# w_up's product by Strassen's seven block products, and w_down as a stage of its own

## Chip and metric

One core of a Trainium2 chip runs one inference step of a decoder layer. The metric is the time of an execution on the device in microseconds. A profile was taken of one further execution; its span, from the first to the last recorded instruction, is what the trace's times count in.

## The reference

Two groups of tokens share the weights: 1024 prompt tokens and 8 x 4 sample tokens, 1056 in all, with 1024 features. Everything is float32. The change concerns the feed-forward part, with d_ff = 2816:

```python
x = x + (g_a * y_a + g_b * y_b + g_m * y_m) @ w_o
h = _rmsnorm(x, norm_ffn_g) @ w_up                        # 1024 -> 2 * 2816
hc, conv_f_state = _causal_dwconv3(h, conv_f_prev, conv_f_w)
hc = hc + conv_f_b
a, gt = jnp.split(hc, 2, axis=-1)
x = x + (jax.nn.silu(gt) * a) @ w_down                    # 2816 -> 1024
```

The convolution runs over three tokens; each sample sequence has two cached rows in front of its four tokens. The final norm follows. Outputs are the normed x and several states, among them the last two rows of h.

## The kernel before

Features lie on the 128 partitions and tokens on the columns. 1056 token columns are cut into three chunks of 352. A float32 operand is kept as two parts of a rounded type (fp32r): hi, which ScalarE casts (L199), and lo, the remainder, which VectorE subtracts (L201). A product is three matmuls for each 128 contracted features (`three`, L221): hi by hi, hi by lo, lo by hi, summed in PSUM.

Weights come in units of 512 KB (8 contracted tiles x 128 columns, or 4 x 256): SP loads one into `ws` (three buffers, L177), it is split into `wh` and `wl`, and `next_unit` and `ahead` (L205, L215) keep up to two split and four loaded ahead. `main` (L239) takes one unit and runs `chunk` (L226) for the three chunks: 24 matmuls of 352 columns into a PSUM tile `mm` (three buffers), then an evacuation by a function that the caller gives. Other work (norms, gates, transposes) is queued in `aux` and woven in between the chunks, by `pace` and `weave` (L99 to L112). Each engine executes its instructions in the order in which the program records them; no scheduler moves them.

The stages around the change are these:

- w_o: 8 units; the first four by `main`, the last four (kept in `kept`) chunk by chunk (L1225 to L1233). `wo_evac` (L1211) adds x, and sums the squares into `acc`. After each chunk its norm (`norm2`, L1196, with `column_norm`, L256) is woven into the next one: a sum over features by PE, a scaling of 8 blocks on VectorE, hi on ScalarE, lo on VectorE and GpSimd in turn.
- w_up: for each of 22 feature tiles j the tile of a and that of the gate, 44 units in all (L1311). `up_evac` (L1243) copies the chunk out of PSUM to `hb`, computes the convolution's centre tap on ScalarE (L1272) and the two others on VectorE (L318), applies the sigmoid (L1280), and the products and the split into hi and lo follow on VectorE and ScalarE (`gate`, L1253).
- w_down: as soon as four tiles j are gated (after j = 4, 8, 12, 16; two after 18), `down_group` (L1296) multiplies them by their rows of w_down and adds the result to S on VectorE (L1294). The last four run at the end in column pieces of 384, 416 and 256, each followed by its final norm and its stores (`finish`, L1345), so that only the last piece's norm is left after the last matmul.

In the w_up part GpSimd sets two zero columns, copies cached columns, and copies the last rows of h (L323, L324, L330, L331). `S` holds x, transposed; `zhi` and `zlo` the parts of the normed x; `fs` and `rs` are pools of 9 and 8 slots of 1088 columns.

Of the kernel before, what the change touches and what calls it, by code (L numbers as in the profile page):

```python
# [31 lines left out]
class Slots:  # L32


    def __init__(self, pool, n, dtype, name):
        self.free = deque(
            pool.tile([P, SLOT], dtype, name=f"{name}{i}", tag=f"{name}{i}") for i in range(n)
        )

    def get(self):  # L40
        return self.free.popleft()

    def put(self, *tiles):
        self.free.extend(tiles)
# [11 lines left out]
def layer_step(ctx: ExitStack, tc: tile.TileContext, I, O):  # L56
# [73 lines left out]
    DOWN = {4: (0, 4), 8: (4, 4), 12: (8, 4), 16: (12, 4), 18: (16, 2)}  # L130
# [24 lines left out]

    def down_units(j0, nk):
        w = 1024 // nk
        for q in range(D // w):
            unit_cols(w_down, q * w, k0=j0, nk=nk, cols=w)

    for j in range(NJ):
        unit_cols(w_up, j * P)
        if j in DOWN:
            down_units(*DOWN[j])
        unit_cols(w_up, FF + j * P)
    for c in range(3):
        down_units(18, 4)
# [199 lines left out]
    with tc.manual_schedule():  # L367
        slots = ctx.enter_context(tc.tile_pool(name="slots", bufs=1))
        fs = Slots(slots, 9, F32, "fs")
        rs = Slots(slots, 8, F32R, "rs")  # L370
# [823 lines left out]
        acc, sqs = fs.get(), fs.get()  # L1194

        def norm2(c):  # L1196
            def sums(ms):
                b = bank()
                for i in range(3):
                    t0, n = PIECES[3 * c + i]  # L1200
                    mmul(b[:n, i : i + 1], lhsT=acc[:, t0 : t0 + n], rhs=ones[:, 0:1], start=True, stop=True)
                for i, n in ((slice(0, 2), P), (slice(2, 3), CH - 256)):
                    nc.vector.tensor_copy(out=ms[:n, i], in_=b[:n, i])
                if c == 2:
                    fs.put(acc)

            total, spread, scales = column_norm(c, G_FFN, sums)
            no = lambda: None
            return [no] * 3 + [total] + [no] * 4 + [spread] + scales

        def wo_evac(f):  # L1211
            def go(c, r, ps):
                until(lambda: c in back)
                nc.vector.tensor_tensor(out=S[:, f, r], in0=ps, in1=S[:, f, r], op=ALU.add)
                if f == 0:
                    nc.scalar.activation(out=acc[:, r], in_=S[:, f, r], func=AF.Square)
                else:
                    i = (f + c) % 3
# [6 lines left out]
        for f in range(4):  # L1225
            main(wo_evac(f))
# [10 lines left out]
        for i in list(kept):  # L1237
            rs.put(*kept.pop(i))
# [222 lines left out]
```

## Time and profile before

| what | value |
|---|---|
| median of 3 runs | 1913.81 us (1911.98 to 1915.22) |
| the profiled execution | 1912.15 us, span 1910.1 us |
| granted TensorE clock | 0.996 of full |
| w_o's matmuls | from about 1034 us |
| w_up and w_down, mixed | about 1129 to 1899 us |
| DMA | 160 MB, mean 84 GB/s |

A row of a group reads: line, engine, operation, result <- operands, shape, count, then busy time and mean length of one in ns, then the idle time of its engine just before and what ended it. A row of the timeline has the start and the length in us first. Lengths of matmuls overlap, as they are pipelined; the distance between two starts is what one costs in a stream. Lengths of VectorE, ScalarE and GpSimd include some start and end that can overlap with the neighbours'. The windows view has the stretch, its length, then busy time of PE, PEld (weight loads), DVE (VectorE), ACT (ScalarE) and POOL (GpSimd), each with a count, the granted clock, the busy share of the DMA engines and GB/s.

### The profile page before, as it was taken

To read this page: it belongs to the slowest core of one execution; us is meant where nothing else is said; L and a number is where in the kernel's file an instruction comes from. 1 tells how busy PE (TensorE), PEld (TensorE's weight loads), DVE (VectorE), ACT (ScalarE), POOL (GpSimd) and SP (SyncE) were. 2 spreads that over 40 slices of the span, in tenths; PEclk is the share of its full clock that TensorE was granted. 3 is DMA by queue.
4 is the path that set the end of the run, shared out by engine and by line. 5 is a ranking of instruction groups with operands and counts; after the bars stand their busy time and mean duration, and the time that the engine had idled before them with its cause. 6 is when DMAs were issued, how large, how long until landed. Compare 5 with 4: busy or idle time off the path is not lost.

```text
span 1910.1 us, 29127 instructions
## 1 busy us (share of the span) xinstructions
PE 1878.9 (98%) x11844; PEld 1856.4 (97%) x11844; DVE 1040.7 (54%) x2274; ACT 631.7 (33%) x1231; POOL 123.8 (6%) x322
## 2 busy tenths in 40 slices
PE   8999999999999999999999999999999999999998
PEld 8988999999999999999999999999999999999997
DVE  5576775336633483329435267546546546556666
ACT  6654313211231123221324144414324324222444
POOL 2231100000000000000000131000000000000000
PEclk9999999999999999999999999999999999999999
DMA  8736152125211432133215001111111111111123
GB/s 263 208 102 219 57 191 67 56 67 167 67 58 45 135 99 70 45 114 119 78 47 181 23 12 56 46 45 45 49 42 45 58 43 46 46 45 48 44 78 135
DMA packets 204851, 160.45 MB, mean 84 GB/s; under 512 B 5477, under 2 KB 191405, under 8 KB 204717
## 3 DMA queue, kind: packets, MB, share of 16 engines
q1 hardware_dynamic: 194660, 144.76, 24.8%
q10 hardware_dynamic: 10057, 13.84, 2.1%
q8 instruction: 93, 1.52, 0.3%
q14 instruction: 41, 0.34, 0.1%
HBM read 144.98 MB, written 13.59 MB: 83 GB/s over the span
## 4 chain that ended last, share of the span: by engine, by line
PE 86%; DVE 7%; issue 3%; ACT 2%; DMA 0%; POOL 0%; DVEq 0%; ACTq 0%; POOLq 0%
PE mm L224 26%; PE mm L222 26%; PE mm L223 26%; DVE qr L855 2%; DVE wl L201 1%; DVE fs L318 1%; PE acc L913 1%; ACT wh L199 1%; PE aux L985 0%; PE aux L986 0%; PE mm L803 0%; PE aux L223 0%; PE aux L984 0%; PE aux L222 0%; PE aux L224 0%
## 5 line engine op out<-in xcount | busy, mean ns | idle before, releaser
L222 PE MATMUL mm<-zhi,wh 128*128 128x352 f32 x2880 | 933.4, 324 | 0.3 <-ACT zhi L284 0.3
L223 PE MATMUL mm<-zlo,wh 128*128 128x352 f32 x2880 | 930.9, 323 | 1.0 <-POOL zlo L295 1.0
L224 PE MATMUL mm<-zhi,wl 128*128 128x352 f32 x2880 | 930.5, 323 | 0.2 <-DVE wl L201 0.2
L222 PEld LDWEIGHTS mm<-zhi,wh 128*128 128x128 f32 x2880 | 542.8, 188 | 1.2 <-ACT zhi L284 0.6
L223 PEld LDWEIGHTS mm<-zlo,wh 128*128 128x128 f32 x2880 | 541.9, 188 | 1.9 <-POOL zlo L295 1.6
L224 PEld LDWEIGHTS mm<-zhi,wl 128*128 128x128 f32 x2880 | 542.0, 188 | 0.5 <-DVE wl L201 0.5
L201 DVE TENSOR_TENSOR wl<-ws,wh 128x1024 fp32r<-128x1024 f32 x181 | 226.6, 1253 | 146.7 <-ACT wh L199 146.5
L199 ACT CAST wh<-ws 128x1024 fp32r<-128x1024 f32 x182 | 190.5, 1049 | 337.8 <-PE mm L223 315.9
L318 DVE SCALAR_TENSOR_TENSOR fs<-fs,vec,fs 128x352 f32<-128x352 f32 (+2 forms) x416 | 199.4, 492 | 98.6 <-ACT fs L1272 88.8
L222 PE MATMUL mm<-rs,wh 128*128 128x352 f32 (+3 forms) x528 | 172.1, 326 | 2.1 <-DVE S L1294 2.1
L223 PE MATMUL mm<-rs,wh 128*128 128x352 f32 (+3 forms) x528 | 171.1, 324 | 0.0
L224 PE MATMUL mm<-rs,wl 128*128 128x352 f32 (+3 forms) x528 | 170.9, 324 | 0.0
L1294 DVE TENSOR_TENSOR S<-mm,S 128x352 f32<-128x352 f32 (+3 forms) x144 | 75.1, 523 | 124.2 <-PE mm L224 124.0
L855 DVE CUSTOM_DVE_ANT_0 qr<-fs,fs 128x256 f32<-128x256 f32 x256 | 108.5, 424 | 7.3
L222 PEld LDWEIGHTS mm<-rs,wh 128*128 128x128 f32 x528 | 99.1, 188 | 3.2 <-ACT fs L360 1.7
L223 PEld LDWEIGHTS mm<-rs,wh 128*128 128x128 f32 x528 | 99.3, 188 | 0.5 <-DVE rs L1261 0.3
L224 PEld LDWEIGHTS mm<-rs,wl 128*128 128x128 f32 x528 | 99.0, 188 | 0.2
L1139 ACT ACTIVATE sig<-mm 128x352 f32<-128x352 f32 x72 | 33.5, 465 | 187.7 <-PE mm L224 187.3
L1271 ACT COPY fs<-mm 128x352 f32<-128x352 f32 (+2 forms) x176 | 62.2, 380 | 91.7 <-PE mm L224 85.1
L1272 ACT ACTIVATE fs<-mm,vec 128x352 f32<-128x352 f32 x132 | 86.7, 656 | 0.0
L1152 DVE TENSOR_TENSOR sig<-sig,fs 128x352 f32<-128x352 f32 x48 | 25.2, 525 | 108.0 <-ACT sig L1139 108.0
L1280 ACT ACTIVATE fs<-fs 128x352 f32<-128x352 f32 x66 | 32.9, 498 | 98.2 <-DVE fs L318 98.1
(235 smaller groups left out, 1561.0 us busy)
## 6 DMA issues: line engine op xcount, KB each, us to landing
ws<-in_w_in SPq DMA_DIRECT2D x88, 512.0 KB
ws<-in_w_up SPq DMA_DIRECT2D x44, 512.0 KB
fs<-q_d SPq DMA_DIRECT2D x32, 512.0 KB
ws<-in_w_down SPq DMA_DIRECT2D x30, 512.0 KB
fs<-in_cache_mem_k SPq DMA_DIRECT2D x16, 512.0 KB
fs<-in_cache_mem_v SPq DMA_DIRECT2D x16, 512.0 KB
xT_d<-S ACTq DMA_DIRECT2D x3, 1408.0 KB
S<-xT_d ACTq DMA_DIRECT2D x6, 704.0 KB
```

Source lines behind the costliest of these rows:

```text
L199: nc.scalar.copy(out=hi, in_=t)
L201: lows.append(lambda: eng.tensor_tensor(out=lo, in0=t, in1=f32(hi), op=ALU.subtract))
L222: mmul(ps, lhsT=wh, rhs=xh, start=first, stop=False)
L223: mmul(ps, lhsT=wh, rhs=xl, start=False, stop=False)
L224: mmul(ps, lhsT=wl, rhs=xh, start=False, stop=last)
L318: nc.vector.scalar_tensor_tensor(out=dst, in0=src(k), scalar=col(w0 + k * step), in1=dst, op0=ALU.mult, op1=ALU.add)
L855: nc.vector.tensor_tensor_reduce(out=att["qr"], in0=q[:, i, :], in1=t[:, 2 * (bb % 2) + mt, :], scale=1.0, scalar=0.0, op0=ALU.mult, op1=A ...
L1139: nc.scalar.activation(out=t, in_=ps, func=AF.Sigmoid)
L1271: nc.scalar.copy(out=dst, in_=src)
L1272: nc.scalar.activation(out=o[:, r], in_=ps, func=AF.Identity, scale=col(CFW + 88 + i), bias=col(CFB + i))
L1280: nc.scalar.activation(out=hold["s"][:, r], in_=o[:, r], func=AF.Sigmoid)
L1294: nc.vector.tensor_tensor(out=S[:, f, r], in0=ps, in1=S[:, f, r], op=ALU.add)
```

## The change

**w_up.** The tokens are cut into four quarters of 264 columns. The weights of an entry are a 2 x 2 block matrix: rows are the tile of a and the tile of the gate of the same j, columns are the two halves of the contracted features (four tiles each). The input is one too: its rows are the two halves of the features, its columns the quarters s and s + 2, with s = 0 or 1. Strassen's scheme, in its form with 15 sums, gives the four output blocks with seven products, numbered 1 to 7 and run in the order 1, 6, 2, 5, 7, 3, 4. One product is 12 matmuls of 264 columns (4 tiles x 3). There are 24 entries: j = 0 and 1 are run for s = 0 alone, then both for s = 1 (entries 0 to 3); from j = 2 on an entry runs both.

- Input sums: `norm2(s)` scales the four blocks, forms four differences of 4 x 264 columns on GpSimd and splits seven operands of that size: hi on ScalarE, lo for six on VectorE and for product 4's on GpSimd. `norm2(0)` is woven into the second half of w_o, `norm2(1)` into entries 0 and 1.
- Weight sums: `w_sum` makes four sums of 512 columns on GpSimd for each entry, three before product 6 and one before product 3; `prepare` casts on ScalarE and takes the lo part on VectorE, or for products 2 and 4 on GpSimd. It runs three products ahead.
- Outputs: `evacuate` adds a product's PSUM tile to a running sum in `S`; seven kinds of additions of 264 columns, 14 on VectorE for a full entry, two copies on ScalarE. `S` is free for this since x goes to DRAM (`x_d`).
- Convolution and gate are done over all 1056 columns at once, as eight `late` items that run during the next entry: for each half centre (ScalarE, with four small GpSimd copies) and two taps (VectorE), then sigmoid (ScalarE, with the product of gate and a on GpSimd) and the gate's last product (VectorE), which is stored to DRAM (`act_d`).

**w_down** begins when w_up is done. For each quarter the gated features are read back from DRAM and split, and for each of four column groups of w_down all 22 tiles are summed in PSUM: w_down is read four times. `finish` takes a quarter in three pieces of 88 tokens.

```diff
+        ORDER = (1, 6, 2, 5, 7, 3, 4)
+        entries = [(0, (0,)), (1, (0,)), (0, (1,)), (1, (1,))] + [(j, (0, 1)) for j in range(2, NJ)]
...
+        def w_sum(e, n):
...
+            if n == 6:
+                tt(out=s1, in0=a21, in1=a22, op=ALU.add)
+                tt(out=s2, in0=s1, in1=a11, op=ALU.subtract)
+                tt(out=a21, in0=a11, in1=a21, op=ALU.subtract)
+                return s2
+            if n == 3:
+                tt(out=a11, in0=a12, in1=s2, op=ALU.subtract)
+                return a11
+            return {2: a12, 5: s1, 7: a21, 4: a22}[n]
...
+        def prepare(upto):
+            while prepared[0] < min(upto, len(steps)):
...
+                a = w_sum(e, n)
+                t = ring.tile([P, KT, P], F32R, name="wh", tag=("wh", "wl")[prepared[0] % 2], bufs=3)
+                hi, lo = t[:, 0:4, :], t[:, 4:8, :]
+                nc.scalar.copy(out=hi, in_=a)
+                eng = nc.gpsimd if n in (2, 4) else nc.vector
+                eng.tensor_tensor(out=lo, in0=a, in1=f32(hi), op=ALU.subtract)
+                wform[e, n] = hi, lo
+                if n == 3 and e + 1 < len(entries):
+                    raw_load(e + 1)
...
+            def sigmoid():
+                s = block(S, j % 2, 1)
+                g = outs[j, 1]
+                nc.scalar.activation(out=s, in_=as4(g), func=AF.Sigmoid)
+                nc.gpsimd.tensor_tensor(out=g[:, :T], in0=g[:, :T], in1=outs[j, 0][:, :T], op=ALU.mult)
+
+            def gate():
+                g, s = outs.pop((j, 1)), block(S, j % 2, 1)
+                nc.vector.tensor_tensor(out=as4(g), in0=as4(g), in1=s, op=ALU.mult)
+                nc.sync.dma_start(out=act_d[j], in_=g[:, :T])
...
+        def product(e, n, s):
+            wh, wl = wform[e, n]
+            ps = banks[s] = bank("mm" if s else "aux")[:, :QC]
+            xh, xl = forms[n, s]
+            for k in range(4):
+                three(ps, wh[:, k, :], wl[:, k, :], xh[:, k, :], xl[:, k, :], k == 0, k == 3)
...
-        for j in range(NJ):
...
+        for at, (e, n) in enumerate(steps):
...
+            prepare(at + 4)
...
+            for _ in range(2 if n == 1 else 1):
+                if late:
+                    late.popleft()()
+            for _ in range(2 if e < 2 else 1):
+                if aux:
+                    aux.popleft()()
+            for s in ss:
+                product(e, n, s)
+            for s in ss:
+                evacuate(e, n, s)
...
+            if 1 in ss:
+                if n == 3:
+                    late.extend(conv_items(j, 0))
+                if n == 4:
+                    late.extend(conv_items(j, 1) + gate_items(j))
...
+        for c in range(4):
...
             for q in range(4):
-                w = next_unit()
+                ps = [bank("mm")[:, :QC] for _ in range(2)]
+                for g in range(6):
+                    wh, wl = next_unit()
+                    ahead()
+                    until(lambda: (c, g) in homes)
```

The next rows are the order of VectorE's queue before, for the second unit of a pair in w_up: L318 are taps, L1256 and L1257 the gate's products, L1261 the low part of the gated features, L201 that of a weight unit.

```order
L318 SCALAR_TENSOR_TENSOR fs_98<-fs_97,vec,fs_98 128x352 x2
L1256 TENSOR_TENSOR fs_98<-fs_98,fs_96 128x352
L1257 TENSOR_TENSOR fs_98<-fs_98,fs_99 128x352
L1261 TENSOR_TENSOR rs_108<-fs_98,rs_110 128x352
L318 SCALAR_TENSOR_TENSOR fs_98<-fs_97,vec,fs_98 128x352 x2
```

And this is VectorE's queue now, in an entry of the later part, from the last tap of the entry before (L1389, L1393) on: L1426 evacuates products 5, then 7, then 3; L1341 are the low parts of the next entry's product 1 (from `ws`) and 6 (from the sum in `S`); L1411 is the gate.

```order
L1389 SCALAR_TENSOR_TENSOR rs_13045<-rs_12912,vec,rs_13045 128x1024
L1393 SCALAR_TENSOR_TENSOR rs_13045<-ext,vec,rs_13045 128x32
L1426 TENSOR_TENSOR S<-aux,S 128x264
L1426 TENSOR_TENSOR S<-mm,S 128x264
L1341 TENSOR_TENSOR wh<-ws,wh 128x512
L1426 TENSOR_TENSOR rs_13181<-aux,S 128x264
L1426 TENSOR_TENSOR S<-aux,S 128x264
L1426 TENSOR_TENSOR rs_13181<-mm,S 128x264
L1426 TENSOR_TENSOR S<-mm,S 128x264
L1341 TENSOR_TENSOR wh<-S,wh 128x512
L1411 TENSOR_TENSOR rs_13045<-rs_13045,S 128x1056
L1426 TENSOR_TENSOR rs_13113<-aux,S 128x264
```

The low part of product 6 stands ahead of the gate and of the evacuations of product 3, and it takes its operand from GpSimd's sum. GpSimd's queue in the same part of w_up was this, for one unit and the beginning of the next:

```order
L323 MEMSET fs_97 128x2
L324 COPY fs_97<-hal_f 128x8x2
L330 COPY tail_f_115<-fs_97 128x2
L331 COPY tail_f_115<-fs_97 128x16
L323 MEMSET fs_103 128x2
```

Now it holds, for an entry, the sum for product 3 (L1325), the low part of 4 (L1341), the product of gate and a (L1407), the three sums for product 6 (L1320 to L1322), the low part of 2 (L1341), and the small copies:

```order
L1325 TENSOR_TENSOR ws<-ws,S 128x512
L1357 MEMSET rs_13113 128x2
L1341 TENSOR_TENSOR wh<-ws,wh 128x512
L1407 TENSOR_TENSOR rs_13045<-rs_13045,fs_12966 128x1056
L1357 MEMSET rs_13181 128x2
L1320 TENSOR_TENSOR S<-ws 128x4x128
L1321 TENSOR_TENSOR S<-S,ws 128x4x128
L1322 TENSOR_TENSOR ws<-ws 128x512
L1341 TENSOR_TENSOR wh<-ws,wh 128x512
L1371 COPY ext<-hal_f 128x8x2
```

What moved: GpSimd's four small operations of a unit became seven operations over 512 or 1056 columns with the small ones beside them, and the sums for product 6 stand behind the product of the entry before, which waits for the sigmoid and so for VectorE's last tap.

More of the change, by code (lines that the diff above doesn't have):

```diff
@@ L1194, in layer_step @@
         acc, sqs = fs.get(), fs.get()
-        def norm2(c):
-            def sums(ms):
-                b = bank()
[L1199 to L1204, printed above, removed]
-                    fs.put(acc)
-            total, spread, scales = column_norm(c, G_FFN, sums)
-            no = lambda: None
-            return [no] * 3 + [total] + [no] * 4 + [spread] + scales
+        QC = 264
@@ new lines, in gate_items @@
+        def gate_items(j):
+            def sigmoid():
[7 more added lines that the diff above has]
+                nc.sync.dma_start(out=act_d[j], in_=g[:, :T])
+                fs.put(g, outs.pop((j, 0)))
+                if j % 4 == 3:
+                    for half in range(2):
+                        aux.append(lambda i=j - 3 + half * NJ, x=2 * half + j // 4 % 2: tail_rows(tail_f[x], i, 4, pf, sf))
+            return [sigmoid, gate]
@@ new lines, in layer_step @@
+        for i, c in enumerate((0, 2, 1, 3)):
+            r = quarter(c)
+            for half in range(2):
+                for f in range(4, 8):
+                    if half == 0:
+                        if f == 4:
+                            nc.sync.dma_start(out=x_d[c, :, 0:4, :], in_=S[:, 0:4, r])
+                        wh, wl = wo[f]
+                        ps = bank("mm")[:, :QC]
+                        for k in range(KT):
+                            three(ps, wh[:, k, :], wl[:, k, :], zhi[:, k, r], zlo[:, k, r], k == 0, k == KT - 1)
+                            if k == 3:
+                                weave()
+                        wo_evac(f)(r, ps)
+                        weave()
+                        nc.sync.dma_start(out=x_d[c, :, f, :], in_=S[:, f, r])
+            if i == 1:
+                prepare(1)
+                aux.extend(norm2(0) + [lambda: prepare(3)])
+                pace(15)
@@ L1337, in layer_step @@
-        for half in range(2):
-            aux.append(lambda i=20 + half * NJ, s=4 + half: tail_rows(tail_f[s], i, 2, pf, sf))
-        gfin = fs.get()
-        nc.sync.dma_start(out=gfin[:, :D], in_=I["norm_final_g"].partition_broadcast(P))
-        nc.scalar.activation(out=one, in_=one, func=AF.Sqrt)
-        def finish(a0, a1, end):
-            rows = [(t, min(P, NP - t)) if t < NP else (t, T - NP) for t in range(a0, a1, P)]
-            banks, ys, sums = {}, {}, {}
+        fs.free.extend(rs.free)
@@ L1349, in finish @@
+        def finish(c, end):
+            rows = [(c * QC + i * 88, 88) for i in range(3)]
+            y = [block(S, h, c) for h in range(2)]
+            banks, yo, sums = {}, {}, {}
             ms, r, tmp = (small.tile([P, 4], F32, name=n, tag=n, bufs=2) for n in ("ms4", "tmp4", "y4"))
@@ L1380, in out @@
                 fr = slice(half * 512, (half + 1) * 512)
[L1381 removed]
+                y, b, ri = yo[i][:n, fr], banks.pop((i, half))[:n, :], r[:n, i : i + 1]
                 if dve:
@@ L1417, in layer_step @@
         drain()
-        for i in range(2):
+        for i in range(3):
             turn(i, 1)()
-        scales(0, 2)
-        for i in range(2):
+        scales(0, 3)
+        for i in range(3):
             out(i, 0, True)
-            out(i, 1, i == 1)
+            out(i, 1, i == 2)
 _INS = [
```

453 lines of the change are left out of this document (311 added, 142 removed).

## The prediction

> **What bounds the kernel now.** I read the page's shares first, then its chain of waits, then the stretch of the FFN in the windows view.
>
> ```profile
> PE 1878.9 (98%) x11844; PEld 1856.4 (97%) x11844; DVE 1040.7 (54%) x2274; ACT 631.7 (33%) x1231; POOL 123.8 (6%) x322
> PE 86%; DVE 7%; issue 3%; ACT 2%; DMA 0%; POOL 0%; DVEq 0%; ACTq 0%; POOLq 0%
> ```
> ```profile
> 1129.00:1892.00 763.00, 760.91 (x4741) 758.68 (x4740) 438.54 (x812) 277.10 (x560) 33.28 (x185) 1.00 0.17 52
> ```
>
> The five busy columns of the window are PE, PEld, DVE, ACT and POOL. From 1129 us w_up and w_down run mixed, and PE rests 2 of 763 us; so PE time removed there is time gained, while nothing else becomes late. VectorE is busy 57% of it, GpSimd 4%. The busy sums say nothing of PE's pace, since matmuls overlap. The pace is the distance of two starts in the timeline:
>
> ```profile
> 1299.78 0.32 PE L223 MATMUL mm<-zlo,wh 128*128 128x352 f32 x1
> 1299.94 0.32 PE L224 MATMUL mm<-zhi,wl 128*128 128x352 f32 x1
> ...
> 1305.86 0.32 PE L222 MATMUL mm<-zhi,wh 128*128 128x352 f32 x1
> ```
> ```profile
> 1883.76 0.28 PE L222 MATMUL mm<-rs,wh 128*128 128x256 f32 x1
> ...
> 1885.08 0.28 PE L224 MATMUL mm<-rs,wl 128*128 128x256 f32 x1
> ```
>
> 38 steps in 6.08 us are 160 ns for 352 columns; 11 steps in 1.32 us are 120 ns for 256. So a column costs 0.417 ns and a matmul 13.3 ns besides; 264 columns take 123.3 ns, an estimate from these two.
>
> **PE's side of the change.** w_up has 44 tiles x 3 chunks x 24 = 3168 matmuls of 352: 506.9 us. The change has 3696 of 264 (seven products x 12 matmuls, once or twice for each of 24 entries): 455.8 us. Gain 51.1. For w_down the old widths stand here:
>
> ```profile
> L222 PE MATMUL mm<-rs,wh 128*128 128x352 f32 x432 | 139.9, 324 | 0.7 <-DVE S L1294 0.7
> L222 PE MATMUL mm<-rs,wh 128*128 128x416 f32 x32 | 11.7, 366 | 0.0
> L222 PE MATMUL mm<-rs,wh 128*128 128x384 f32 x32 | 11.0, 344 | 1.4 <-DVE S L1294 1.4
> L222 PE MATMUL mm<-rs,wh 128*128 128x256 f32 x32 | 9.5, 296 | 0.0
> ```
>
> Three lines each: 1296 x 160 ns + 96 x (187 + 173 + 120) ns = 253.5 us; now 22 x 8 x 4 x 3 = 2112 x 123.3 = 260.4, a loss of 6.9. Half of w_o goes from 288 matmuls of 352 to 384 of 264, a loss of 1.3. PE alone therefore gains 42.9 us: Strassen removes an eighth of the work (63 us), and 20 us go back to the 13.3 ns of more and narrower matmuls. [...]
>
> **What else an entry asks for.** These are the prices for VectorE, ScalarE and GpSimd:
>
> ```profile
> L900 DVE TENSOR_TENSOR rs<-fs,rs 128x512 fp32r<-128x512 f32 x32 | 21.6, 690 | 5.0 <-ACT rs L899 5.0
> L642 DVE SCALAR_TENSOR_TENSOR fs<-fs,r,fs 128x512 f32<-128x512 f32 x16 | 11.3, 749 | 0.4
> L318 DVE SCALAR_TENSOR_TENSOR fs<-fs,vec,fs 128x352 f32<-128x352 f32 x208 | 120.2, 584 | 59.5 <-ACT fs L1272 54.5
> L318 DVE SCALAR_TENSOR_TENSOR fs<-fs,vec,fs 128x32 f32<-128x32 f32 x104 | 26.0, 250 | 2.7
> L676 DVE TENSOR_TENSOR S<-aux,S 128x256 f32<-128x256 f32 x32 | 13.6, 425 | 1.1
> L201 DVE TENSOR_TENSOR wl<-ws,wh 128x1024 fp32r<-128x1024 f32 x181 | 226.6, 1253 | 146.7 <-ACT wh L199 146.5
> L1383 DVE SCALAR_TENSOR_TENSOR fs<-aux,tmp,fs 128x512 f32<-128x512 f32 x14 | 9.9, 745 | 0.2
> L646 POOL TENSOR_TENSOR rs<-fs,rs 128x512 fp32r<-128x512 f32 x16 | 20.3, 1292 | 98.8 <-ACT rs L645 73.8 <-PE aux L617 12.5 <-PE aux L671 12.5
> L201 POOL TENSOR_TENSOR wl<-ws,wh 128x1024 fp32r<-128x1024 f32 x1 | 2.4, 2362 | 8.9 <-ACT wh L199 8.9
> L324 POOL COPY fs<-hal_f 128x16 f32<-128x16 f32 x44 | 11.9, 270 | 0.2 <-POOL fs L323 0.2
> L899 ACT CAST rs<-fs 128x512 fp32r<-128x512 f32 x32 | 19.0, 619 | 19.6 <-PE acc L913 15.4 <-DVE wl L201 4.2
> L1272 ACT ACTIVATE fs<-mm,vec 128x352 f32<-128x352 f32 x132 | 86.7, 656 | 0.0
> L1280 ACT ACTIVATE fs<-fs 128x352 f32<-128x352 f32 x66 | 32.9, 498 | 98.2 <-DVE fs L318 98.1
> L199 ACT CAST wh<-ws 128x1024 fp32r<-128x1024 f32 x182 | 190.5, 1049 | 337.8 <-PE mm L223 315.9 <-DMA ws<-in_w_o 4.2 <-issue 3.2
> ```
> ```profile
> 1894.49 1.41 DVE L1383 SCALAR_TENSOR_TENSOR fs<-aux,tmp,fs 128x512 f32<-128x512 f32 x2
> ```
>
> A full entry gives PE 168 x 123.3 ns = 20.7 us. VectorE gets 14 evacuations (0.43), 5 low parts (0.69), 4 taps (1.28 extended from 352 and 512 columns, plus 0.25 for the sample columns) and a gate (1.28): 16.9 us, less 0.08 where one follows another (the pair above takes 1.41 for 2 x 0.745), about 14.7. GpSimd gets 4 sums and 2 low parts (1.29), a product of 1056 (2.43) and 8 small copies (0.25): 12.2 us, after 33 in the whole FFN before. ScalarE has 7 casts, two centres (1.23), a sigmoid (1.08) and two copies, under 9 us. Each fits beside 20.7. They are queued in order, though, and VectorE waits twice: its low part of product 6 stands behind a chain of sigmoid 1.08, GpSimd's product 2.43, two sums 2.58 and a cast 0.62, 6.7 us after the last tap, of which the two evacuations of product 5, one low part and the four of product 7 fill 2.7: 4.0 us idle, with the gate and the evacuations of products 3 and 4 queued behind, for which PE waits three banks later. The low part of product 5 waits for the centre and its cast, 1.85 less two evacuations: 1.1. So 19.8 us, and some 0.4 for eight handovers: 20.2, still just under PE.
>
> **The shared cost.** The trace shows what happens when both engines combine two SBUF tensors:
>
> ```profile
> 101.94 2.52 POOL L646 TENSOR_TENSOR rs<-fs,rs 128x512 fp32r<-128x512 f32 x2 [4.44 <-ACT rs L645]
> 123.55 2.55 POOL L646 TENSOR_TENSOR rs<-fs,rs 128x512 fp32r<-128x512 f32 x2 [8.46 <-ACT rs L645]
> ```
> ```profile
> 103.51 2.04 DVE L201 TENSOR_TENSOR wl<-ws,wh 128x1024 fp32r<-128x1024 f32 x1 [1.64 <-ACT wh L199]
> 117.49 1.22 DVE L201 TENSOR_TENSOR wl<-ws,wh 128x1024 fp32r<-128x1024 f32 x1
> 123.85 0.42 DVE L676 TENSOR_TENSOR S<-aux,S 128x256 f32<-128x256 f32 x1
> ```
>
> GpSimd is done at 104.46, and the VectorE low part that began at 103.51 ends at 105.55, 1.09 later; alone it takes 1.22. It stood still while GpSimd ran. The evacuation at 123.85, with one operand in PSUM, ran beside GpSimd at its usual 0.42. In an entry GpSimd meets such VectorE work four times: the third sum before the low part of 6 (0.5), its own low part of 2 before the gate (1.2), the sum for 3 before the low part of 5 (1.1), its low part of 4 among the taps (1.2). If all four meet, an entry takes 24.2 us; if the gate and evacuations slip in first, 20.2, and then PE's 20.7 holds. I take the middle, 22.3, since evacuations are a third of VectorE's work: 1.6 us over PE in each of 20 full entries, **+32** (bounds 0 and +70). No row of before shows a tap held like a low part. [...]
>
> The two norms scale blocks of 264 columns; the row for 352 gives 0.48 us for one:
>
> ```profile
> L281 DVE SCALAR_TENSOR_TENSOR fs<-S,vec,aux 128x352 f32<-128x352 f32 x48 | 25.9, 574 | 5.3 <-PE aux L272 5.3
> ```
>
> **Start.** Entries 0 to 3 are half entries, 41.4 us of PE together, with full weight sums and the second input norm in them: GpSimd 24 x 1.29 + 6 x 2.43 + 2 = 47.6 us; VectorE work of the held kind 20 x 0.69 + 6 x 1.28 + 6.1 + 1.3 = 28.9. Side by side that is 6 us over PE, one after the other 35. The first norm's chain is woven into 23 us of w_o matmuls: sixteen scalings of 0.48 and, if they never overlap, five GpSimd operations of 2.43, three sums and VectorE's six low parts of 1.28, 31.4 us, so up to 9 more.  I take **+26** (6 to 44). **Passage to w_down.** After the last product come taps 5.8, sigmoid, product, gate 4.8, a store and a load, cast and low part 1.9. The end of the program bounds a DMA:
>
> ```profile
> 1905.76 0.66 DVE fs L1383
> ```
>
> From 1906.4 the last store has 3.7 us to the span's end; with two such, 19.9 us, against 120 matmuls for the first 20 tiles, 14.8: **+5**, up to +12 with the weight units' low parts between. **w_down** reads its weights four times, 96 units, some 62 MB with the activations in 260 us. The nearest row is w_k and w_v, also a 512 KB unit every 3 to 4 us:
>
> ```profile
> 110.00:172.00 62.00, 59.72 (x327) 51.54 (x326) 47.98 (x92) 30.47 (x47) 11.18 (x9) 1.00 0.48 154
> ```
>
> 2.3 of 62 us idle would be 10 us of 260; the old w_down idles none; I take **+3**. The act stores sit on SP between weight loads and wait for the gate; a load behind them has an entry to land. The final norm has three pieces of 88 instead of two: **+1**.
>
> **Sum.** -42.9 + 32 + 26 + 5 + 3 + 1 = +24. The profiled execution took 1912.15 us (span 1910.1); that gives 1936, and as the median of 3 is 1.7 above it, I say 1938 for the median.
>
> **Rivals.**
> 1. *PE stays the bound* (faster). The meetings fall under evacuations, entries take 20.7, start +10, passage and w_down +6: 1912 - 43 + 17 = 1886. For it: no engine exceeds 17 us an entry. Against: VectorE's queue, in its order, has half a microsecond of slack an entry, and GpSimd is at work 12 of 20.7 us with the very kind of operation that held it up. It decides at about 21.1 us an entry: below, the change gains. Chance 0.27.
> 2. *The two engines meet every time* (much slower): 24.2 an entry and one after the other at the start, -43 + 70 + 44 + 15 = 1998. For it: once VectorE is late it no longer waits for PE, so its held operations follow one another just when GpSimd's are due. Against: a third of its work comes from PSUM and ran undisturbed. Chance 0.13.
> 3. *Even*: about 21.1 an entry, 1914: what PE gains is just eaten up. Chance 0.07.
> 4. *Fewer products than told, or more*: the program lists 3696 matmuls of 264 in the stage, so under 0.01.
>
> My forecast has 0.53. Faster by over 0.2% (3.8 us, about what a measurement of this kernel can tell) 0.27, within it 0.07, slower 0.66. The range leaves out the far ends of the first two rivals: 1885 to 1980.
>
> **What would show it.** Right: PE idle within the w_up stage, ended by VectorE's low parts or GpSimd's sums; an entry at 22 to 24 us; VectorE low parts and taps longer than 0.69 and 1.28; starts of 264-column matmuls 123 ns apart where they run freely; the first four entries near 67 us. [...]

## The result, and the profile after

The changed kernel takes 2017.1 us (2014.6 to 2018.3) against 1913.7, a ratio of 1.054 (95% interval 1.0525 to 1.0556): slower, as forecast, but by 103 us where 24 were forecast. The profiled execution has a span of 2012.8 us. One run below, late_group, had a mean granted clock of 0.83 where the other changed kernels have 0.97 to 0.99, so its time is not compared with theirs. The changed kernel's page, busy times and granted clock:

```profile
PE 1872.2 (93%) x13032; PEld 1834.4 (91%) x13032; DVE 1169.2 (58%) x2307; ACT 673.4 (33%) x1122; POOL 408.8 (20%) x531
PEclk9999999999999999999999779999999998899999
```

PE was busy 98% before, and its clock stood at full rate through the FFN (1.00 from 1129 to 1892 us). Now PE is idle for 7% of the span, and the clock drops in slices 23 and 24 and again in 34 and 35 of the 40 (1107 to 1208 us and 1661 to 1761 us), where w_up and w_down begin. To see which stage holds the idle time I cut the windows view at matmuls that can be counted (384 of 264 columns belong to w_o, 84 to a half entry, 168 to a full one, 528 to a quarter of w_down). W_o's first matmul stands at 1025.7 us here and at 1027.5 us before, not at the 1034 of the table further up. The rows are w_o with the first norm, entries 0 to 3, entries 4 to 23, w_down, the end; columns as in the prediction, with the clock behind the five engines:

```profile
1025.70:1142.50 116.80, 97.51 (x712) 96.96 (x711) 48.17 (x75) 29.66 (x49) 33.36 (x27) 0.93 0.24 81
1142.50:1219.60 77.10, 55.44 (x350) 51.85 (x351) 55.97 (x81) 26.64 (x41) 41.57 (x37) 0.82 0.20 54
1219.60:1693.30 473.70, 431.28 (x3372) 420.82 (x3371) 338.36 (x558) 162.07 (x253) 255.13 (x342) 0.98 0.24 71
1693.30:1999.80 306.50, 279.56 (x2200) 276.26 (x2199) 173.60 (x237) 131.94 (x174) 6.38 (x13) 0.94 0.67 214
1999.80:2012.80 13.00, 1.71 (x14) 1.20 (x12) 4.45 (x13) 3.41 (x9) 2.52 (x2) 0.77 0.28 83
```

PE's pace in undisturbed stretches of w_up, from the timeline:

```profile
1262.39 0.29 PE L211 MATMUL aux<-zlo,wh 128*128 128x264 f32 x1
...
1263.60 0.28 PE L212 MATMUL aux<-zhi,wh 128*128 128x264 f32 x1
```

Ten steps in 1.21 us are 121 ns (forecast 123.3). With 121 ns for 264 columns and 160 for 352, the stages need 92.5 (288 x 160 + 384 x 121 ns), 40.7, 406.6 and 255.6 us of PE:

| | forecast | measured |
|---|---|---|
| PE's own work | -43 | -57 |
| w_o and entries 0 to 3 over PE | +26 | 24.3 + 36.4 = +60.7 |
| 20 full entries over PE | +32 | +67.1 |
| passage and w_down over PE | +8 | +50.9 |
| the rest (13.0 at the end; before, 30.1 over PE in all, from w_o's first matmul on) | +1 | -17 |
| sum | +24 | +105 |

W_o began those 1.8 us earlier than before, which leaves the 102.7 us by which the spans differ.

**A full entry** takes 23.7 us (473.7 / 20). VectorE in that stage was busy 338.4 us, 16.9 an entry, and it waited for one thing only:

```profile
DVE wh L1341 <- ACT wh L1339: 135.6, 40, 6.6
```

That is 6.8 an entry, and 16.9 + 6.8 = 23.7: VectorE, working or waiting, fills the entry and sets its length. There are two waits an entry: one before the low part of product 6, 4.4 us in nearly every entry, and one before that of product 5, 1.17 us in 14 of 20. One wait of the first kind in the timelines of ScalarE, GpSimd and VectorE (start, length, instruction):

```profile
1312.03 1.09 ACT L1406 ACTIVATE S<-fs 128x1056 f32<-128x1056 f32 x1 [5.43 <-DVE fs L1393]
1318.37 0.62 ACT L1339 CAST wh<-S 128x512 fp32r<-128x512 f32 x1 [5.25 <-POOL S L1321]
```
```profile
1313.19 2.47 POOL L1407 TENSOR_TENSOR fs<-fs,rs 128x1056 f32<-128x1056 f32 x1 [5.20 <-ACT S L1406]
...
1315.66 1.30 POOL L1320 TENSOR_TENSOR S<-ws 128x512 f32<-128x512 f32 x1
1317.04 1.29 POOL L1321 TENSOR_TENSOR S<-S,ws 128x512 f32<-128x512 f32 x1
1318.29 1.28 POOL L1322 TENSOR_TENSOR ws<-ws 128x512 f32<-128x512 f32 x1
1319.59 1.68 POOL L1341 TENSOR_TENSOR wh<-ws,wh 128x512 fp32r<-128x512 f32 x1
```
```profile
1314.15 0.42 DVE L1426 TENSOR_TENSOR S<-mm,S 128x264 f32<-128x264 f32 x1
1319.02 1.10 DVE L1341 TENSOR_TENSOR wh<-S,wh 128x512 fp32r<-128x512 f32 x1 [4.44 <-ACT wh L1339]
1320.04 2.34 DVE L1411 TENSOR_TENSOR fs<-fs,S 128x1056 f32<-128x1056 f32 x1
1322.31 0.42 DVE L1426 TENSOR_TENSOR rs<-aux,S 128x264 f32<-128x264 f32 x1
```

It is the chain of the prediction: sigmoid, GpSimd's product, two sums, cast. VectorE stands 4.44 us; then its low part takes 1.10 (0.68 alone) and its gate 2.34 (1.25 alone) beside GpSimd's work; the evacuations for which PE waits come after both. Taps are held as well, which no row of before could show (minimum, median, maximum; then one case of each engine):

```profile
L1389 DVE SCALAR_TENSOR_TENSOR rs<-rs,vec,rs x52: 1270/1274/2312, 1213.4 to 1714.7; 128x1024 f32<-128x1024 f32 x52
L1393 DVE SCALAR_TENSOR_TENSOR rs<-ext,vec,rs x64: 237/244/1300, 1215.6 to 1715.9; 128x32 f32<-128x32 f32 x64
```
```profile
1351.44 1.28 POOL L1341 TENSOR_TENSOR wh<-ws,wh 128x512 fp32r<-128x512 f32 x1 [2.96 <-ACT wh L1339]
1351.47 1.30 DVE L1393 SCALAR_TENSOR_TENSOR rs<-ext,vec,rs 128x32 f32<-128x32 f32 x1
```

The tap that is held is mostly the small one over the 32 sample columns: it meets GpSimd's low part of product 4 and takes 1.27 to 1.30 us in place of 0.24 in 14 of the 20 full entries. Of the 88 large taps one is held, at 2.31 in place of 1.27. Counted over their shortest lengths, the held low parts, gates and small taps add 16.2, 16.3 and 14.3 us to the 20 entries, 2.3 an entry.

**The start** has one long stall of PE, for the sums of the second norm:

```profile
1141.57 1.04 PE L1219 MATMUL aux<-ones,fs 128*88 128x1 f32 x6 [17.53 <-DVE fs L1286]
1142.47 0.57 PE L210 MATMUL aux<-zhi,wh 128*128 128x264 f32 x1
1142.84 0.42 PE L211 MATMUL aux<-zlo,wh 128*128 128x264 f32 x1
1143.06 0.42 PE L212 MATMUL aux<-zhi,wh 128*128 128x264 f32 x1
```
```profile
1127.07 3.37 DVE L1251 TENSOR_TENSOR fs<-S,fs 128x1056 fp32r<-128x1056 f32 x1 [1.45 <-ACT fs L1250]
...
1139.00 1.09 DVE L1341 TENSOR_TENSOR wh<-S,wh 128x512 fp32r<-128x512 f32 x1 [5.51 <-ACT wh L1339]
...
1140.99 0.52 DVE L1286 TENSOR_TENSOR fs<-fs,fs 128x264 f32<-128x264 f32 x1 [0.55 <-ACT fs L1284]
```
```profile
1126.20:1141.00 14.80, 0.00 (x0) 0.00 (x0) 6.85 (x7) 4.81 (x8) 10.75 (x7) 0.50 0.05 18
1143.00:1146.00 3.00, 3.00 (x16) 3.00 (x15) 1.10 (x7) 0.66 (x3) 0.00 (x0) 0.50 0.37 112
```

The last sum of w_o (L1286) stood in VectorE's queue behind the first norm's low parts (L1251, one of them 3.37 us long where the shortest take 1.25) and the low part of product 6 (L1341), which waited 5.5 us for the cast of GpSimd's sum. While PE stood the granted clock fell to 0.50, and the matmuls after it came 0.22 us apart in place of 0.121. So this wait cost more than its length; the prediction had no term for that.

**w_down.** PE's longest waits from 1693 us on:

```profile
PE mm L210 <- ACT fs L1516: 9.8, 1, 9.8
PE aux L1584 <- DVE fs L1610: 6.1, 2, 3.6
PE mm L212 <- DVE wl L189: 3.8, 1, 3.8
PE mm L211 <- DVE fs L1517: 2.9, 1, 2.9
```

By counted matmuls its four quarters take 87.9, 73.2, 72.0 and 73.4 us for 63.9 of PE.

### The profile page after: what moved, and what is told of

Same layout as the page of the kernel before. It is cut to its first block, busy times and chain, and to the rows that moved or that the text cites. A ratio compares the mean times of both kernels' runs of the same rounds, so it can differ in the third digit from the quotient of the medians.

```text
span 2012.8 us, 32245 instructions
## 1 busy us (share of the span) xinstructions
PE 1872.2 (93%) x13032; PEld 1834.4 (91%) x13032; DVE 1169.2 (58%) x2307; ACT 673.4 (33%) x1122; POOL 408.8 (20%) x531
## 5 line engine op out<-in xcount | busy, mean ns | idle before, releaser
L210 PE MATMUL mm<-zhi,wh 128*128 128x352 f32 (+1 forms) x2656 | 835.0, 314 | 4.4 <-DVE rs L1426 2.6
L211 PE MATMUL mm<-zlo,wh 128*128 128x352 f32 (+1 forms) x2656 | 831.0, 313 | 1.4 <-POOL zlo L283 1.0
L212 PE MATMUL mm<-zhi,wl 128*128 128x352 f32 (+1 forms) x2304 | 729.1, 316 | 3.9 <-DVE wl L189 3.9
L212 PEld LDWEIGHTS mm<-zhi,wl 128*128 128x128 f32 x2304 | 437.2, 190 | 4.5 <-DVE wl L189 4.4
L189 DVE TENSOR_TENSOR wl<-ws,wh 128x1024 fp32r<-128x1024 f32 (+1 forms) x203 | 244.8, 1208 | 216.1 <-ACT wh L187 215.7
L1341 DVE TENSOR_TENSOR wh<-S,wh 128x512 fp32r<-128x512 f32 x48 | 52.7, 1098 | 157.5 <-ACT wh L1339 157.5
L210 PE MATMUL mm<-fs,wh 128*128 128x264 f32 x280 | 84.9, 303 | 35.1 <-DVE rs L1426 20.1
L210 PE MATMUL aux<-zhi,wh 128*128 128x264 f32 x352 | 104.3, 296 | 10.9 <-ACT fs L348 5.9
L212 PE MATMUL aux<-zhi,wh 128*128 128x264 f32 x352 | 103.1, 293 | 3.4 <-DVE wh L1341 3.4
L211 PE MATMUL aux<-zlo,wh 128*128 128x264 f32 x352 | 102.5, 291 | 0.0
L212 PE MATMUL mm<-zhi,wh 128*128 128x264 f32 x352 | 100.7, 286 | 0.0
L1341 POOL TENSOR_TENSOR wh<-ws,wh 128x512 fp32r<-128x512 f32 x48 | 74.4, 1551 | 79.4 <-ACT wh L1339 75.3
L210 PE MATMUL aux<-fs,wh 128*128 128x264 f32 x264 | 78.0, 296 | 10.4 <-ACT wh L1339 9.0
L212 PE MATMUL aux<-fs,wh 128*128 128x264 f32 x264 | 78.6, 298 | 9.6 <-DVE wh L1341 9.2
L211 PE MATMUL mm<-fs,wh 128*128 128x264 f32 x280 | 82.8, 296 | 2.9 <-DVE fs L1517 2.9
```

The lines of the kernel that those rows point to most:

```text
L189: lows.append(lambda: eng.tensor_tensor(out=lo, in0=t, in1=f32(hi), op=ALU.subtract))
L210: mmul(ps, lhsT=wh, rhs=xh, start=first, stop=False)
L211: mmul(ps, lhsT=wh, rhs=xl, start=False, stop=False)
L212: mmul(ps, lhsT=wl, rhs=xh, start=False, stop=last)
L1341: eng.tensor_tensor(out=lo, in0=a, in1=f32(hi), op=ALU.subtract)
```

## Experiments

Theory A: VectorE's queue stands behind GpSimd's chain. Theory B: the time in which the two engines hold each other up sets the entry. Theory C: tail rows (the last rows of h, transposed by PE, copied by ScalarE and stored, after each fourth feature tile), stores and DMAs do. D to H concern w_down and the start, T the tail rows' banks; each is stated with its run. Runs with one time have 1912 to 1915 us for the kernel before beside them.

**chain_cut.** Product 6 takes a raw block in place of its sum, so the kernel's result is another; all sums are still made.

```
             if n == 6:
...
-                return s2
+                return a22
```

> GpSimd keeps all its work (four sums, two low parts and a product an entry), but the weight form of product 6 is cast from a raw block, so VectorE's low part of it no longer waits for sigmoid, product and two sums; product 6 then multiplies another block. Theory A (VectorE's queue stands behind that chain): the 4.4 us waits before this low part go, full entries fall from 23.7 to about 21.5 us, the time by 35 to 45 us to about 1975. Theory B (the two engines hold each other up, whoever waits): GpSimd's work and its meetings stay, entries stay above 23 us, the time falls by less than 12 us. Theory C (PE's waits come from the tail rows' copies, the stores and the DMAs): no change, within 4 us of 2017.

**no_sums.** The four weight sums are left out and raw blocks multiplied, so this result is another too.

```
-                tt(out=s1, in0=a21, in1=a22, op=ALU.add)
...
-            return {2: a12, 5: s1, 7: a21, 4: a22}[n]
+            return {6: a22, 2: a12, 5: a21, 7: a21, 4: a22}[n]
```

> All four weight sums of an entry are left out, the products multiply raw blocks; GpSimd keeps two low parts, the product and the small copies, 7 us an entry in place of 12. Theory A: as without the chain, entries near 21.5 us and, since the start's sums go too, the time 40 to 60 us lower, but little below the run without the chain in the full entries (under 0.5 us each). Theory B: the meetings halve, full entries fall well below those of the run without the chain, by 1 us or more. Theory C: only the start gets shorter, by at most 15 us.

1975.5 and 1933.9 us. The full entries in the windows view, without the chain and without sums:

```profile
1219.10:1654.30 435.20, 419.05 (x3372) 412.49 (x3370) 369.08 (x558) 159.90 (x251) 301.54 (x342) 1.00 0.26 78
```
```profile
1206.40:1617.90 411.50, 410.13 (x3372) 409.70 (x3371) 340.20 (x563) 162.57 (x253) 147.60 (x264) 1.00 0.28 84
```

Cutting only the wait takes 38.5 us off the stage, as A said, with GpSimd's work kept. Yet VectorE's busy time rises from 338 to 369 us for the same 558 instructions: it now works while GpSimd does, and is held (18 of the 88 large taps, where one was). Without the sums it is 340, and the stage falls another 23.7 us, to 20.6 an entry where PE alone needs 20.3. So A carries the larger part. The rest goes with GpSimd's sums, but not to B alone: half of it, 12 us, lies in the five entries with tail rows, 23.0 us each with the sums made and 20.6 without them. C falls as the main cause: without the sums an entry with tail rows is only 0.1 us longer than the others.

**sums_early** and **quarter_loads**: the same without leaving work out.

```
-            if n == 6:
+            if n == (1 if e else 6):
                 tt(out=s1, in0=a21, in1=a22, op=ALU.add)
```
```
+            for x in names:
+                t = spare.popleft()
...
+                    raw_load(e + 1, *{1: (2, 3), 7: (0,), 3: (1,)}.get(n, ()))
...
-        r = fs.get()
+        r = small.tile([P, P], F32, name="tr", tag="tr", bufs=1)
```

> The three sums for product 6 of the next entry are issued one weight form earlier, ahead of the gate's product in GpSimd's queue, so that they are done before the sigmoid is; nothing is left out. Theory A: the wait before the low part of product 6 goes as in the run without the chain, entries near 21.5 us, the time 30 to 45 us lower. Theory B: same work, same meetings at other moments, under 12 us. If the raw blocks have not landed by then (their load starts two steps before), GpSimd waits for the DMA and the gain is smaller: 10 to 20 us.

> Nothing is left out. The raw weights of an entry come in four blocks of 256 KB, each into a buffer as soon as one is free, so that the three blocks that the early sums read are there two steps before them (with the sums early but whole loads, GpSimd waited 86.6 us for them); and the tail rows are copied to a tile of their own in place of a slot that the next conv buffer takes while its store still reads it. Theory A (the chain): full entries near 21.7 us as in the run without the chain, the time 35 to 45 us below 2017, at 1972 to 1982. Theory B (the engines' meetings): entries stay above 22.5 us, the time above 1990. Tail rows: if GpSimd's waits for their stores make the fourth entry longer, it falls from 26 us to within 1 us of the others.

2000.1 us for the first: the wait had moved to GpSimd, whose sums now came before their weights:

```profile
POOL S L1318 <- DMA ws<-in_w_up: 86.6, 19, 5.7
```

1966.9 us for the second, 50 below the changed kernel; the full entries:

```profile
1214.60:1649.10 434.50, 420.57 (x3372) 415.34 (x3371) 401.51 (x562) 161.05 (x253) 284.02 (x340) 0.99 0.25 77
```

The same stage time as with the chain cut, so the order of GpSimd's queue was the cause of that part. VectorE is busy 401 us there, 61 more than without sums, and yet nine entries take 20.4 us; the five with tail rows take 24 to 25. The tail rows' own tile did not shorten it: my expectation for that was wrong.

**stores_pool** and **norm_spread**: two edits for quarters 1 to 3 of w_down.

```
-                queue = nc.sync if dve else nc.scalar
+                queue = (nc.sync if dve else nc.scalar) if end else nc.gpsimd
```
```
-                    if q == 0 and g == 5:
+                    if c == 0 and q == 0 and g == 5:
                         drain()
```

> The output stores of the first three token quarters go out on GpSimd's queue, idle in w_down, instead of SyncE's, where weight loads of w_down stand behind them. Bytes and work are the same. Theory D (SyncE's queue stands behind stores that wait for the norm's results): ScalarE's 42 us of waits for w_down weights fall below 20, quarters 1 to 3 fall from 73 to about 68 us each, the time by 10 to 20 us. Rival E (the DMA bandwidth of 62 MB in 260 us): the waits and the quarters stay, the time within 4 us.

> Nothing is left out. The final norm of a token quarter is no longer drained at the sixth weight unit of the next quarter, but its pieces alternate with the activation loads and splits over the whole quarter. Theory F (the burst holds the weight casts behind it on ScalarE and VectorE, and PE's transposes for its banks): quarters 1 to 3 fall from 73 to 66 to 68 us each, the time by 12 to 20 us. Rival E (weights cannot come faster): they stay at 71 to 73 us, the time within 4 us.

2012.0 and 2016.2 us, where 10 to 20 us less were expected. The quarters stay at 71 to 73 us in both. ScalarE's waits for w_down weights in quarters 1 to 3 fell from 29.4 to 18.1 us with the stores moved, without helping PE: D falls. Spreading the norm took away PE's waits for the transposes' banks and put others in their place:

```profile
PE mm L210 <- DVE S L1679: 11.9, 11, 2.7
```

Each output pair now waited for an evacuation (L1679) behind the spread work in VectorE's queue, with three banks for pairs of two.

**late_group.**

```
+            return every[0:5] + every[6:11] + [every[5]] + every[11:] if c == 0 else every
```

> Nothing is left out. In the first token quarter of w_down the sixth group of activations, which waits for the last gate, comes after five groups each of two output pairs in place of one. Theory H (the passage waits for the chain of taps, sigmoid, product, gate, store and load): the waits of 10 and 3.5 us go and the first quarter falls from 88 to 72 to 77 us, the time by 11 to 16 us. Rival (the weight units' casts are the late ones there): the quarter stays above 83 us.

Its time, 2100.5 us, is not compared; the order of its waits can be read. PE's wait did not go:

```profile
1786.65 0.59 PE L210 MATMUL mm<-fs,wh 128*128 128x264 f32 x1 [11.37 <-ACT fs L1516]
```
```profile
1783.61 1.08 ACT L1406 ACTIVATE S<-rs 128x1056 f32<-128x1056 f32 x1 [3.13 <-DVE rs L1393]
...
1785.53 1.07 ACT L1516 CAST fs<-S 128x1056 fp32r<-128x1056 f32 x1
```

The matmul waits for the fourth group's split, which stands behind the last sigmoid in ScalarE's queue, and that waits for VectorE's taps. H was wrong: PE waited not for the sixth group's chain but for a step queued behind it.

**no_early_forms.**

```
-                aux.extend(norm2(0) + [lambda: prepare(3)])
+                aux.extend(norm2(0))
```

> Nothing is left out. The first weight forms of products 6 and 2 are no longer prepared ahead of w_o's last sums, but when the entries begin. Theory G (PE's 17.5 us stall before the second input norm comes from VectorE's queue, where w_o's last sum stands behind the low part of product 6, idle 5.5 us for it): w_o's second half falls from 70 to 62 to 65 us and most of it stays, the time 4 to 8 us lower. Rival (GpSimd's work at the start is the bound): the same wait comes back before product 6 in the first entry, the sum of w_o and the four half entries within 2 us of 147.5.

2011.5 us; w_o's second half falls from 70.4 to 60.6, the half entries rise from 77.1 to 85.6. The sum is 1.3 us less: the rival was right, the wait only moved.

**start_vector** and **down_order.**

```
-        b = bank()
+        b = bank("acc" if cnt == 4 else "aux")
...
-            dve, pool = nc.vector, nc.gpsimd
+            dve, pool = nc.vector, nc.vector
```
```
-        rest = [*late, splits[3], loads[5], splits[4], splits[5]]
+        rest = [*late[:2], splits[3], *late[2:5], splits[4], *late[5:], loads[5]]
...
+                    pss[q] = [bank(x)[:, :QC] for x in ("mm", "acc" if q % 2 else "mm")]
```

> Nothing is left out. As the run with quarter loads, and two edits more. The three differences and the low part that GpSimd makes in each input norm go to VectorE (1.26 us there by the rows of the changed kernel, 2.4 or more on GpSimd). Theory L (at the start the two engines run one after the other, so the sum of their times counts): w_o's second half and the four half entries, 141.7 us together, fall by 6 to 14 us. Rival (VectorE's queue is the longer one, GpSimd's share was hidden): they stay or grow by up to 5 us. And the tail rows' transposes get the PSUM bank that nothing else uses there. Theory T (their bank is one of the four that the products take in turn, so that the next product waits for an evacuation): each fourth full entry falls from 24 to 25 us to 21 to 21.5, 15 us in all. Rival (the transposes and their copies cost that much themselves): it stays. With both theories 1938 to 1948 us.

> Nothing is left out; only w_down is changed. The fourth and fifth group's splits stand ahead of the last sigmoid in ScalarE's queue, the sixth group is multiplied after five groups of two output pairs, x and the norm's gain are loaded later. Theory H2 (PE's 10 us wait was for the fourth group's split, which stood behind that sigmoid): the first quarter falls from 88 to 72 to 77 us. Rival (the weight units come late there, the queue being full of act and x loads): above 82 us. In quarters 1 to 3 the norm is spread as before, but the output pairs no longer take three banks in turn. Theory F2 (spreading failed since PE then waited 1 to 3 us at each pair for a bank): 73 to 67 to 69 us each. Rival E (casts and weights): 71 us or more. With both theories the time is 24 to 32 us lower, at 1985 to 1993.

1964.8 us: w_o's second half 65.8 instead of 70.4, the half entries 71.8 instead of 71.3; 4.1 us where 6 to 14 were expected. The fourth entries stayed at 24 to 26: PE's second tail transpose now waited for ScalarE's copy out of the one bank. 2000.4 us for down_order; its w_down:

```profile
1695.50:1985.70 290.20, 274.29 (x2201) 271.58 (x2200) 171.31 (x237) 130.16 (x174) 8.48 (x13) 0.98 0.70 226
```

16.3 us less: 80.0, 72.6, 69.3 and 68.3 by quarters. H2 and F2 hold in part.

**all_fixes** and **all_fixes_2.**

```
+        for c in (0, 1):
...
+                wo_block(w, f, c, ahead)
+                wo_block(w, f, c + 2)
...
+        aux.extend([lambda: None] * 8 + norm2(1))
```
```
+        for h in range(2):
+            nc.tensor.transpose(b[:72, h * P : (h + 1) * P], srcs[h].rearrange("p k i -> p (k i)"), ident)
+        nc.scalar.copy(out=r[:72, : 2 * P], in_=b[:72, : 2 * P])
```

> Nothing is left out. The edits that helped together (early sums, quarter loads, norms on VectorE, the order of w_down), with three more: w_o does all its output tiles for quarters 0 and 2 before those for 1 and 3, so that the first input norm has 46.8 us of PE beside it in place of 23.4 (four weight units are loaded twice); the second norm's sums come after four products of the first entry; both tail rows go through one bank and one unused block. If the start is short of cover (PE's 14 to 17 us stall is w_o's last sum behind the norm in VectorE's queue), w_o's second half and the half entries, 137.6 us in the last run, become 112 to 122 us. If each fourth entry is long for the tail rows' banks and copies, it falls from 25 to 21. Then with w_down at 288 the time is 1905 to 1918, about the kernel before. Rival: the norms' own work on VectorE sets the start, which stays above 130, and the time at 1925 or more.

> Nothing is left out. As the run before, with two mends: the two tail rows of a fourth entry are both transposed ahead of one copy of both (in the run before, PE's second transpose waited 3 to 5 us for ScalarE's copy of the first, in each of five entries), and the fifth group's split in w_down stands before the last taps. Theory T2 (the fourth entries are long only for that wait): they fall from 25 to 29 us to 20.5 to 21.5, 30 us in all, and the time to 1908 to 1916, even with the kernel before (ratio 0.997 to 1.002). Rival (the copies' and stores' time on ScalarE holds the weight casts behind them): they stay at 23 us or more, the time above 1922.

1942.3 us, then 1927.5 (median of five; ratio to before 1.0076, interval 1.0062 to 1.009); 1905 to 1918 and 1908 to 1916 were expected. With twice the cover, and the norms' GpSimd work on VectorE, w_o runs at PE's pace; the first row of all_fixes, and in its timeline what a tail row still cost:

```profile
1027.20:1123.10 95.90, 95.90 (x797) 95.90 (x796) 49.76 (x84) 31.34 (x53) 18.96 (x22) 1.00 0.41 129
```
```profile
1260.47 0.40 PE L346 MATMUL acc<-ident,tail_f 128*72 128x128 f32 x1 [5.10 <-ACT S L348]
```

The start, with 46.5 us for half of w_o taken off as in the runs before, is 124 us where I expected 112 to 122: the half entries stay at 74.6. In all_fixes_2 the tail row's wait is gone: the fourth entries fall from 25 to 29 us to 21 to 22. The others, though, rise from 20.4 to 21.2:

```profile
1197.90:1622.70 424.80, 417.55 (x3372) 412.63 (x3371) 401.00 (x558) 159.28 (x246) 277.19 (x339) 1.00 0.25 78
```

VectorE is busy 94% of this stage. It seems that the long fourth entries had let it catch up; no run tests that alone. The other edit of all_fixes_2, the fifth group's split ahead of the last taps, did not help: w_down takes 291.1 us in place of 286.9, its first quarter 84.5 in place of 78.0.

**vector_lows, act_queue, both_moves.**

```
-                eng = nc.gpsimd if n in (2, 4) else nc.vector
-                eng.tensor_tensor(out=lo, in0=a, in1=f32(hi), op=ALU.subtract)
+                nc.vector.tensor_tensor(out=lo, in0=a, in1=f32(hi), op=ALU.subtract)
...
-                nc.gpsimd.tensor_tensor(out=g[:, :T], in0=g[:, :T], in1=outs[j, 0][:, :T], op=ALU.mult)
+                nc.vector.tensor_tensor(out=g[:, :T], in0=g[:, :T], in1=outs[j, 0][:, :T], op=ALU.mult)
```
```
-                    nc.sync.dma_start(
+                    nc.gpsimd.dma_start(
                         out=z[:, :nk, :], in_=act_d[k0 : k0 + nk, :, quarter(c)].rearrange("k p t -> p k t")
...
```

> Nothing is left out. As all_fixes_2, but the two low parts and the gate's product that GpSimd makes in an entry go to VectorE; GpSimd keeps the four sums and the small copies, 7 us an entry in place of 12, and VectorE has 17.2 in place of 14.7. Theory B2 (work of the two engines on two SBUF operands excludes each other, so the sum of it sets the entry): by the rows the held work of both falls from 22.0 to 19.5 us, full entries from 21.2 to 20.4 to 20.6, the four half entries from 74.6 to 64 to 70, the time from 1927 to 1903 to 1912. Rival (VectorE's queue is the bound by itself): entries grow to 21.5 us or more, the time to above 1932.

> Nothing is left out. As all_fixes_2, but w_down's activation and x loads and the stores of its first three quarters go through GpSimd's queue, and only weights are left on SyncE's. Theory D2 (weight loads stand behind activation loads that wait for the last gate): ScalarE's waits for w_down weights in the first quarter go, it falls from 84.5 to 68 to 73 us, the time by 10 to 16 us. Rival E2 (the loads themselves are late when weights, activations and x come at once): the first quarter stays above 80 us.

> Nothing is left out. Both edits. If both theories hold they add up, the stages being apart: 1887 to 1900 us, below the kernel before (ratio 0.987 to 0.994). If only the first holds, 1903 to 1912 (0.995 to 1.0); if only the second, 1911 to 1917.

1925.7, 1925.1 and 1924.6 us (the last a median of five, ratio 1.0064, interval 1.005 to 1.0078). The full entries of vector_lows:

```profile
1199.10:1620.60 421.50, 418.44 (x3372) 411.42 (x3371) 409.30 (x621) 159.14 (x246) 164.91 (x277) 1.00 0.25 79
```

GpSimd's 112 us less bring 3.3 us at most: an entry takes 21.1, neither B2's 20.5 us nor the rival's 21.5, and the half entries stay (76.6 where 64 to 70 were expected). Between act_queue and both_moves, whose w_up differs by the same edit, the stage does not change (422.9 and 423.1). VectorE is busy 97% of it now, so its own work is the bound. In act_queue ScalarE's waits for w_down's weights fall from 49.4 to 21.6 us, but w_down stays (291.7 against 291.0; its first quarter 81.2 against 84.5, the second 75.4 against 69.6). D2 falls. No version gets below the kernel before.

## Why the prediction was right in sign and wrong in size

- **PE's side** held: 121 ns for 123.3, a gain of 57 for 43.
- **The entry's mechanism** held, and most of its sizes: VectorE busy 16.9 us an entry, against 14.7 and a middle hold of 2.1. All four meetings take place, each for less than its full price or not in every entry, 2.3 in all where four full ones would be 4.0; the middle was a choice without a row behind it, so that it came out near is luck. Nor had the 1.2 us for taps in the four a row of before behind it; in the changed kernel the held small taps cost 14.3 us in 20 entries, 0.7 an entry. The waits before the low parts of products 6 and 5 are 4.4 and 1.17 in most entries (forecast 4.0 and 1.1). The step that failed is that the tail rows have no term. In five entries the wait before the low part of 5 is 5.3 to 5.7. One of them, on VectorE, on ScalarE and its queue, and on GpSimd:

```profile
1397.06 0.69 DVE L1341 TENSOR_TENSOR wh<-S,wh 128x512 fp32r<-128x512 f32 x1 [5.30 <-ACT wh L1339]
```
```profile
1393.65 1.27 ACT L1376 ACTIVATE fs<-rs,vec 128x1056 f32<-128x1056 f32 x1 [3.39 <-DMA act_d<-fs]
...
1395.10 0.64 ACTq L350 DMA_DIRECT2D out_new_conv_ffn_prompt<-rs  x1
1395.77 0.59 ACTq L350 DMA_DIRECT2D out_new_conv_ffn_sample<-rs  x1
1396.40 0.62 ACT L1339 CAST wh<-S 128x512 fp32r<-128x512 f32 x1 [1.33 <-issue]
```
```profile
1397.72 0.10 POOL L1357 MEMSET rs<- 128x2 f32 x1 [3.77 <-DMA out_new_conv_ffn_sample<-rs]
```

  ScalarE's cast for product 5 stands behind a centre that waits 3.4 us for the gate's store to leave its slot, and behind the issue of the tail rows' two stores, 1.3 us. GpSimd waits for a tail store too, but later (to 1397.72), so that is not what holds VectorE here. The centre waits for a gate's store in these five entries only, where the tail rows take a slot of the pool from which it gets its own. Five such waits are 21 us above the usual 1.17, or 1.05 an entry: most of the 1.3 by which the waits, 6.8 an entry, exceed the 5.1 and 0.4 of the forecast. So an entry took 23.7 for 22.3, 28 us in 20 entries, and since PE ran faster than I reckoned (20.3 for 20.7), the stage lies 67 and not 32 over it.
- **"I take the middle, 22.3, since evacuations are a third of VectorE's work"** put the loss down to the engines' meetings, with 20.2 us without it. The runs turn that round: the queue's wait is the larger part (38.5 us), and that of the meetings the smaller (23.7 at most, as GpSimd's work went with the sums and half of it lies in the entries with tail rows). In the changed kernel the two engines meet less because one waits for the other: VectorE is busy 338 us there, and 369 in chain_cut, where it waits less.
- **Start: "so up to 9 more"** was the first norm's own excess; the stage had 24, and the +26, with the first four entries "near 67 us", leaves it next to nothing. I added durations and forgot whose queue they stand in: w_o's last sums came behind the norm, and PE's next instruction, the second norm's sum, needs them. More cover, with the norms' GpSimd work on VectorE, removed it (95.9 us for all of w_o, 116.8 in the changed kernel). The half entries took 77.1 for 67; without sums they took 67.2, so GpSimd's sums, and who waits for them, cost 10 us there. What makes up their other 26 us over PE is open.
- **Passage +5, w_down +3**, the largest miss: 24 over PE in the first quarter, 27 in the others. I reckoned DMA and the last chain, and gave the order of ScalarE's and VectorE's queues no term. The runs found a split queued behind the last sigmoid, and PE's waits for banks that the norm's pieces hold; changing the order took 16.3 us off, and moving stores or activation loads to another queue took off 2.2 at most. Some 31 us over PE stay in the best order (286.9 us in all_fixes), and their cause is not settled.
- **No term for the clock.** Of the matmuls of 264 columns, 301 are followed by the next after 0.18 to 0.27 us instead of 0.121. Of these, 222 began while the granted clock was 0.50, and they took 22 us more than at 0.121; the other 79, at full clock, 8. This is part of the excesses above, not added to them.
- Of the rivals, the even case and the faster one fell; 1998, both engines meeting every time, came nearest by its number, but not by its mechanism. Of what was to show it right, the held low parts, the waits before them and the pace were there, and of the taps mostly the small ones were held; the mean entry lies within 22 to 24 us; the first four entries were not near 67. Waits for w_down's weights showed on ScalarE (42 us), hardly on PE.

## What to carry to other kernels

When work moves to another engine, follow the in-order queue of each engine that waits for it, not only the sums of durations: here 4.4 us of waiting an entry, at one place in VectorE's queue, made 38.5 of a stage of 474 us, and issuing three sums one step earlier, with their operands there in time, gave back as much. A removed wait shows the next limit, so look at busy shares again after each step: VectorE went from 71% to 94% by losing its waits. Arithmetic saved on PE counts only as far as a second engine has room for the additions that buy it, and here the start and the passage, which the kernel before had mixed with other work, cost 61 and 51 us over PE.

## What the runs showed of the hardware

PE's granted clock was 1.00 in the window 1123.0 to 1126.0 us and 0.50 from 1126.2 on, 2.4 us after the start of its last instruction before the long stall (1123.82). It was still 0.50 in the window to 1146.0, after work had come back at 1141.6, with the matmuls 0.22 us apart, and 1.00 in the window 1147.0 to 1150.0. Two shorter waits differ: PE idled 1.97 us from 1386.35 on, and from 1388.9 to 1392.3 the granted clock was 0.50, the matmuls again 0.22 us apart; after 1.96 us from 1292.09 on it stayed at 1.00. GpSimd too took longer when the engines met: its low part took 1.68 us beside VectorE's gate (the row at 1319.59) and 1.27 at its shortest. A VectorE instruction of 0.24 us took 1.30 us beside a GpSimd one of 1.28 (the rows at 1351.47 and 1351.44), 1.06 more, so even a small instruction was dear there.
